# Dealing row pairs in turn to sixteen partition groups in a SwiGLU kernel: a 16 x 8 access pattern in place of 128 rows

## The chip, the cores and the metric

The kernel runs on one core of one Trainium2 chip. The metric is the device time of one execution in microseconds. Before the change the median is 936.3 us (936.06 to 936.35 in three runs). The kernel moves 268.44 MB from HBM into SBUF and 134.22 MB back, so it is a question of transfers almost alone (the two queues' shares of sixteen engines' span, 68.6 and 31.2%, add up to 99.8%). In this program HBM is the memory that holds x and out; SBUF is the one that holds the tiles, 128 partitions (rows) on which SiLU and the multiply work. A transfer (DMA) between the two is issued from a queue, here SP's or ACT's. The profile's page reckons the shares of the queues on sixteen DMA engines, and the records show each transfer as packets: here one packet is the run of one partition (3,968 load packets of 65,536 bytes, 31 loads of 128 partitions). A transfer has landed when its last packet is in place.

Runs are sorted by a rule into fast and slow: a run over 1.5% above the fastest of the same kernel counts as slow. A ratio is the mean time of one kernel's fast runs over that of the kernel before's fast runs in the same rounds, so it is not quite the ratio of the medians that I quote. Where only one run of a kernel counts as fast there is no ratio.

## The reference

```python
def reference(x):                     # x: [8192, 8192] float32
    a, b = np.split(x, 2, axis=-1)
    silu_b = b / (1 + np.exp(-b))
    return a * silu_b                 # [8192, 4096] float32
```

## The kernel before

A tile takes 256 rows. Each of the 128 partitions holds two neighbouring rows, 64 KiB of x in one run, and writes two result rows, 32 KiB of out in one run. Three such tiles fill 192 KiB of each partition. Loads are issued from the SP queue, stores from the ACT queue, the last ones from SP.

```python
    R = 2
    BUFS = 3
    xv = x.tensor.reshape([N // R, R * M]).ap()         # row pairs of x, 64 KiB each
    ov = out.tensor.reshape([N // R, R * half]).ap()    # row pairs of out, 32 KiB each
    ntiles = N // (P * R)                               # 32
    ...
    def load(i, rows=None):
        ...
        nc.sync.dma_start(
            out=tiles[i][:, lo * M : hi * M], in_=xv[i * P : (i + 1) * P, lo * M : hi * M]
        )
    ...
    def store(i, c0=0, cw=R * half):
        (nc.scalar if i < last - 1 else nc.sync).dma_start(
            out=ov[i * P : (i + 1) * P, c0 : c0 + cw], in_=tiles[i][:, c0 : c0 + cw]
        )

    for i in range(BUFS):
        load(i)
    for i in range(last):
        for k in range(R):
            swiglu(i, k)          # SiLU in place on ACT, then the multiply on DVE
        ...
        store(i)
        nxt = i + BUFS
        if nxt < last:
            load(nxt)
    ... # the last tile is loaded in two halves and stored in two halves
```

## Time and profile before

| | kernel before |
|---|---|
| span in the profile | 934.8 us |
| 64 KiB load packet, median of the packet records | 2.42 us |
| 32 KiB store packet, median of the packet records | 1.21 us |

The prediction below shows the engine totals, the queues, the chain and the stretches. Here are the rates of the forty slices and the issues of the large transfers from the page of the kernel before. In an issue line the last number is the median time from issue to landing.

```profile
GB/s 404 400 445 430 430 439 433 428 435 443 428 430 439 429 442 432 435 426 453 419 430 452 411 452 423 428 447 425 433 433 453 414 443 429 426 447 428 425 437 376
...
out_dram<-xt ACTq DMA_DIRECT2D x30, 4096.0 KB, 39.7
...
xt<-in_x_dram SPq DMA_DIRECT2D x31, 34.5
```

The first two slices, nearly all loads (the first store packet starts at 39.5 us, the slices end at 46.7), run at 404 and 400 GB/s; after that the rate stands near 433. A load takes 34.5 us to land. The middle of the run handles one tile in 29.0 us (for example, the chain's loads start at 98.96, 185.89 and 272.94 us, three tiles apart). So when the next load is issued, only some 34.5 - 29.0 = 5.5 us of loading is still queued (my estimate).

### The profile page before, as it was taken

Reading aid. Unit: us, or ns where it says so; the run is one execution under the profiler, and the core shown is the slowest. Engines: PE = TensorE matmul, PEld = TensorE weight load, DVE = VectorE, ACT = ScalarE, POOL = GpSimd, SP = SyncE. Lnnn points to the kernel's source line nnn. Section 1 sums busy time; section 2 is a strip of 40 time slices with the busy share of each in tenths; the row PEclk is TensorE's granted clock in tenths of the full one; section 3 lists DMA queues with packets and bytes.
Section 4 is the critical chain, followed back from the end, with each engine's and each line's share of the span. In section 5 each row is a group of like instructions: output and inputs, shape, how many; then the busy total and the mean of one; then the engine's idle time right before and its main releaser. Section 6 shows DMA issues by size and latency. Waiting matters only on the chain.

```text
span 934.8 us, 367 instructions
## 1 busy us (share of the span) xinstructions
DVE 283.3 (30%) x65; ACT 229.4 (25%) x66; POOL 0.2 (0%) x4
## 2 busy tenths in 40 slices
DVE  0333312333123331133321333213332133331242
ACT  0223320233302333113331133311333203332041
POOL 0000000000000000000000000000000000000000
DMA  9999999999999999999999999999999999999998
GB/s 404 400 445 430 430 439 433 428 435 443 428 430 439 429 442 432 435 426 453 419 430 452 411 452 423 428 447 425 433 433 453 414 443 429 426 447 428 425 437 376
DMA packets 9506, 402.67 MB, mean 431 GB/s; under 512 B 1056, under 2 KB 1056, under 8 KB 1056
## 3 DMA queue, kind: packets, MB, share of 16 engines
q1 hardware_dynamic: 5184, 276.83, 68.6%
q10 hardware_dynamic: 4320, 125.83, 31.2%
q14 instruction: 2, 0.02, 0.0%
HBM read 268.44 MB, written 134.22 MB: 431 GB/s over the span
## 4 chain that ended last, share of the span: by engine, by line
DMA 84%; DVE 10%; ACT 4%; DVEq 0%; issue 0%; SPq 0%; ACTq 0%
DMA out_dram<-xt 42%; DMA xt<-in_x_dram 42%; DVE xt L51 10%; ACT xt L50 4%; DVEq L106 0%; SPq L43 0%; ACTq L50 0%; DVEq L51 0%
## 5 line engine op out<-in xcount | busy, mean ns | idle before, releaser
L51 DVE TENSOR_TENSOR xt<-xt 128x4096 f32<-128x4096 f32 (+1 forms) x65 | 283.3, 4359 | 637.7 <-ACT xt L50 634.5
L50 ACT ACTIVATE xt<-xt 128x4096 f32<-128x4096 f32 (+1 forms) x65 | 228.1, 3556 | 688.1 <-DMA xt<-in_x_dram 688.1
L50 ACT ACT_TABLE_LOAD x1 | 1.3, 1283 | 0.7 <-PEq L95 0.7
L95 POOL MEMSET const-bfloat16-1.0<- 128x1 bf16 x1 | 0.1, 103 | 0.0
L95 POOL MEMSET const-uint8-127<- 128x1 uint8 x1 | 0.1, 102 | 0.0
L95 POOL MEMSET const-float32-0.0<- 128x1 f32 x1 | 0.1, 100 | 0.2 <-issue 0.2
L95 POOL MEMSET const-float32-1.0<- 128x1 f32 x1 | 0.1, 99 | 0.0
## 6 DMA issues: line engine op xcount, KB each, us to landing
out_dram<-xt ACTq DMA_DIRECT2D x30, 4096.0 KB, 39.7
xt<-in_x_dram SPq DMA_DIRECT2D x2, 4096.0 KB, 27.1
out_dram<-xt SPq DMA_DIRECT2D x1, 4096.0 KB, 23.6
out_dram<-xt SPq DMA_DIRECT2D x2, 2048.0 KB, 14.5
xt<-in_x_dram SPq DMA_DIRECT2D x31, 34.5
```

The source lines that it names most:

```text
L50: nc.scalar.activation(out=b, in_=b, func=_SILU)
L51: nc.vector.tensor_mul(out=xt[:, k * half + c0 : k * half + c0 + cw], in0=xt[:, k * M + c0 : k * M + c0 + cw], in1=b,)
L95: nc = _bacc.Bacc("TRN2", target_bir_lowering=False, num_devices=1)
```

## The change

The intent is to bring together in HBM what is read at the same moment. Before, a partition group of eight reads eight consecutive row pairs, so groups are 512 KiB apart in x and 256 KiB apart in out. After, consecutive row pairs are dealt in turn to the sixteen groups, so groups are 64 and 32 KiB apart. Each partition still has one 64 KiB run and one 32 KiB run per tile, and the result is the same.

```diff
-    xv = x.tensor.reshape([N // R, R * M]).ap()
-    ov = out.tensor.reshape([N // R, R * half]).ap()
     ntiles = N // (P * R)
+    G = 16
+    xv = x.rearrange("(i j e r) m -> i e j (r m)", i=ntiles, e=G, r=R)
+    ov = out.rearrange("(i j e r) m -> i e j (r m)", i=ntiles, e=G, r=R)
...
-            out=tiles[i][:, lo * M : hi * M], in_=xv[i * P : (i + 1) * P, lo * M : hi * M]
+            out=tiles[i][:, lo * M : hi * M], in_=xv[i, :, :, lo * M : hi * M]
...
-            out=ov[i * P : (i + 1) * P, c0 : c0 + cw], in_=tiles[i][:, c0 : c0 + cw]
+            out=ov[i, :, :, c0 : c0 + cw], in_=tiles[i][:, c0 : c0 + cw]
```

In the built program this does two things at once. The HBM addresses change, and the HBM side of each transfer becomes a pattern of 16 x 8 rows instead of 128 rows. The second was not the intent.

## The prediction

A "pair" is two engines that hinder each other when they work on like packets at the same moment ("in step"), each then taking twice as long. That was an assumption; no trace had shown it. So were two others: that a pair's lag at the start would last, and that a lag of four packets would cost nothing. The sum of the forecast came to 188 + 558 + 560 = 1,306, rounded to 1,300 us. All three terms can be read below (the case without cost: 937 to 950 us, taken as 942 in the first term), and the ground of the other two is the assumption just named. "HBM aliasing" stands for load packets that grow longer by the spacing of the addresses; no trace had shown that either. The chance of 0.01 for a gain of over 2% rested on the ceiling; what the trace shows is 433 GB/s with the engines occupied for 99.8% of the span.

> **What bounds the kernel now.** I read the engine totals first, then the slices, the queues, the chain that ended last, and last a table of stretches, to see whether some part of the run is unlike the rest.
>
> ```profile
> DVE 283.3 (30%) x65; ACT 229.4 (25%) x66; POOL 0.2 (0%) x4
> ...
> DMA  9999999999999999999999999999999999999998
> ...
> DMA packets 9506, 402.67 MB, mean 431 GB/s; under 512 B 1056, under 2 KB 1056, under 8 KB 1056
> ## 3 DMA queue, kind: packets, MB, share of 16 engines
> q1 hardware_dynamic: 5184, 276.83, 68.6%
> q10 hardware_dynamic: 4320, 125.83, 31.2%
> ```
>
> The compute engines work 30% and 25% of the span, while the DMA row is full in every slice. The two queues together occupy 68.6 + 31.2 = 99.8% of sixteen engines' span: 933 of 934.8 us. Nothing that shortens a wait can give more than the missing 2 us; only faster packets could.
>
> How fast are the packets? Queue 1 holds 0.686 x 16 x 934.8 = 10,260 engine-us for 276.83 MB, 27.0 GB/s per engine; queue 10 holds 4,667 engine-us for 125.83 MB, also 27.0 GB/s. One queue mostly reads HBM, the other only writes it, and their rates are equal. The single packet records say it more sharply: a 65,536-byte load packet takes 2.42 us at the median, a 32,768-byte store packet 1.21 us, and only 38 of the 8,192 row packets are over 20 ns longer than the usual time for their size, most of them at the first tile or near 49 us. [...]
>
> ```profile
> by line: DMA out_dram<-xt 42.5%; DMA xt<-in_x_dram 41.5%; DVE xt L51 9.7%; ACT xt L50 4.1%; issue 0.2%; DVEq L106 0.2%; SPq L43 0.1%; ACTq L50 0.0%; DVEq L51 0.0%
> ```
>
> The chain of waits passes load, SiLU, two multiplies, store, and back to the load that needed the buffer. Its 14% of compute is no gain in reserve: other tiles' transfers fill the engines in that time.
>
> ```profile
> 60.00:500.00 440.00, 132.76 (x30) 106.84 (x30) 0.00 (x0) 1.00 1.00 433
> 500.00:890.00 390.00, 115.05 (x26) 94.60 (x27) 0.00 (x0) 1.00 1.00 433
> 890.00:935.00 45.00, 17.77 (x5) 12.44 (x5) 0.00 (x0) 1.00 0.93 399
> ```
>
> In these lines the last two columns are the DMA share and GB/s. The middle of the run is even: 433 GB/s with the engines wholly occupied.
>
> [...]
>
> **The change, part by part.** The instruction order on all engines is unchanged: 33 loads, 33 stores, 65 SiLUs and multiplies, the same sizes and waits. A partition still holds one 64 KiB run of x and writes one 32 KiB run of out, so I expect the same 8,192 row packets and 9,506 in all, and 0 us for compute and issue.
>
> What is meant to change is which HBM rows are read together. That can remove at most the excess of slow packets: summed over the 38 and divided by 16 engines, it is 2.2 us. So the gain side is worth 0 to 2 us.
>
> What the change also does, beside the pitch, is to alter the form of the access pattern. In the built kernel the DRAM side is no longer 128 rows but 16 x 8 rows, against 128 partitions in SBUF. [...]
>
> The cost depends on how far a pair is out of step. In the steady part an engine alternates one load packet L (2.42 us) and one store packet S (1.21 us): 3.63 us, 256 such pairs being the floor of 929 us. I assume [...] that only like meets like. Then:
> - in step: L takes 4.84 and S 2.42, 7.26 for 3.63, twice the time: 929 x 2 = 1,858, about 1,865 us with the ends.
> - out of step by a lag between S and L, 1.2 to 2.4 us: L covers 2/3 of each period, so two L's overlap for at least 1/3 of it, 1.21 us, which adds 1.21: 4.84 for 3.63, times 1.33: about 1,240 us.
> [...]
>
> [...] The packets of the first wave start within 0.8 us of each other, and a lag of 0.5 us costs (7.26 - 1.0)/3.63 = 1.72. Over hundreds of packets lags should drift, and the slowest pair sets when a tile has landed. [...]
>
> **The rivals.**
> - Nothing happens: [...] the pairs drift fully apart at once. For it: the kernel already overlaps three tiles with no barrier between packets, and the first wave (packets up to 3.47 us) settled to 2.42 us after one packet. [...] It gives 934 to 950 us; chance 0.2.
> - HBM aliasing: [...] If it came anyway, load packets alone 5 to 20% longer would add 0.05 to 0.2 x 600 = 30 to 120 us (600 being 3,968 load packets x 2.42 / 16): 965 to 1,055. Chance of it alone about 0.1.
> - The change gains what its author hoped: at most 2 us, to 934; under 2% in any case.
> - Transfer issue becomes dearer with three dimensions: the store issue takes 0.34 us on ACT's queue now; doubled over 33 stores it is 11 us, off the path while other packets are queued. It moves nothing.
>
> **Range and chances.** I weigh no meeting 0.2 at 942 us, the 1.33 case (with weaker meeting or aliasing beside it) 0.45 at 1,240, and near step 0.35 at 1,600: 188 + 558 + 560 = 1,306, rounded to 1,300 us. The distribution has two humps, and the range must reach both: 940 to 1,750. Faster by over 2% would need 917 us, or 402.65 MB at 439 GB/s[...]: 0.01. Within 2%: 0.19. Slower: 0.80.
>
> **What would show it.** Right: packets and bytes the same, DMA row still full, SiLU and multiply as long as now (3.6 and 4.4 us), but load packets of 3 to 4.8 us and stores of 1.6 to 2.4 us in the records, steady GB/s of 220 to 330, and long packets all through the run rather than a few at its start. [...] Times of 2.42 and 1.21 throughout prove the first rival[...]. A packet count other than 9,506 would show that the rows are cut differently, which I have not counted on. The prediction fails most cheaply at the lag: if pairs separate by themselves within a few tiles, the answer is some 945 us[...].

## The result, and the profile after

The changed kernel takes 1,548.22 us in the median of six runs (1,513.63 to 1,560.27) against 936.24 us. The ratio of the fast runs is 1.626 (1.615 to 1.638). The result is correct.

The profile fell on the longest of the six runs (span 1,558.5 us). These lines are from the page of the changed kernel: engine totals, the DMA row of the slices and their rates, the queues, and the issues.

```profile
DVE 283.2 (18%) x65; ACT 229.4 (15%) x66; POOL 0.2 (0%) x4
...
DMA  9999999999999999999999999999999999999997
GB/s 215 215 267 278 254 259 258 262 267 262 252 259 272 256 262 275 241 272 253 277 254 264 254 264 266 267 246 268 255 271 257 266 248 275 249 272 259 262 243 236
DMA packets 9506, 402.67 MB, mean 258 GB/s; under 512 B 1056, under 2 KB 1056, under 8 KB 1056
...
q1 hardware_dynamic: 5184, 276.83, 77.9%
q10 hardware_dynamic: 4320, 125.83, 21.6%
...
out_dram<-xt ACTq DMA_DIRECT2D x30, 4096.0 KB, 59.7
...
xt<-in_x_dram SPq DMA_DIRECT2D x31, 71.9
```

Compute is unchanged to 0.1 us, and so are the packets and the bytes, to the packet. The DMA row is as full as before. A busy share therefore tells nothing here: the engines are occupied in both kernels, but the packets last longer. The loads' queue pays most: 68.6% of 934.8 us was 641 us of each engine, 77.9% of 1,558.5 is 1,214 us. The stores' queue went from 292 to 337 us. Those two add 573 + 45 = 618 us, nearly the whole 624 us by which the spans differ.

In the packet records a 64 KiB load packet now takes 4.64 us on average, 1.92 times the former 2.42. A 32 KiB store packet on the ACT queue takes 1.40 us, 1.16 times the former 1.21. The first two slices, loads alone until the first store packet at 67.3 us, are the plainest reading: 215 GB/s, about half of the 404 and 400 GB/s of the same slices before and of the 433 of the middle of that run. In them the load packets after the first wave take about 5.1 us, 2.1 times the former 2.42. (A slice counts a packet whole where it starts; sixteen packets of 65,536 bytes in 5.12 us are 205 GB/s.)

The table of stretches of the changed kernel (last two columns: DMA share and GB/s) shows that the loss is even over the run:

```profile
60.00:300.00 240.00, 44.24 (x10) 35.61 (x10) 0.00 (x0) 1.00 1.00 262
600.00:900.00 300.00, 53.10 (x12) 42.73 (x12) 0.00 (x0) 1.00 1.01 263
1200.00:1500.00 300.00, 61.95 (x14) 48.56 (x14) 0.00 (x0) 1.00 1.00 261
```

The chain of waits is of no use in this profile. It gives 94% to a releaser that it can't name:

```profile
another core or an unknown queue 94%; DMA 3%; SPq 1%; ACT 0%; DVE 0%; DVEq 0%; issue 0%; ACTq 0%
```

There is no other core in this program. The SP queue's own waits are readable instead (waited for, us in total, times, longest):

```profile
SPq L44 <- DMA out_dram<-xt: 1443.8, 29, 110.3
```

Loads still wait for the stores that free their buffers, as before, where the same wait was:

```profile
SPq L43 <- DMA out_dram<-xt: 869.3, 29, 67.8
```

No new wait was formed; the same loop turns more slowly.

### The profile page after: what moved, and what is told of

The parts are those of the page before. It is cut to its first block, busy times and chain, and to the rows that moved or that the text cites. A ratio compares the mean times of both kernels' runs of the same rounds, so it can differ in the third digit from the quotient of the medians.

```text
span 1558.5 us, 367 instructions
## 1 busy us (share of the span) xinstructions
DVE 283.2 (18%) x65; ACT 229.4 (15%) x66; POOL 0.2 (0%) x4
## 2 busy tenths in 40 slices
DMA packets 9506, 402.67 MB, mean 258 GB/s; under 512 B 1056, under 2 KB 1056, under 8 KB 1056
## 3 DMA queue, kind: packets, MB, share of 16 engines
q1 hardware_dynamic: 5184, 276.83, 77.9%
## 4 chain that ended last, share of the span: by engine, by line
another core or an unknown queue 94%; DMA 3%; SPq 1%; ACT 0%; DVE 0%; DVEq 0%; issue 0%; ACTq 0%
DMA xt<-in_x_dram 3%; SPq L44 1%; ACT xt L51 0%; DVE xt L52 0%; DVEq L107 0%; ACTq L51 0%
## 6 DMA issues: line engine op xcount, KB each, us to landing
out_dram<-xt ACTq DMA_DIRECT2D x30, 4096.0 KB, 59.7
```

## The experiments

My theory was that in the 16 x 8 form DMA engines hinder each other in pairs when they work at the same moment, and that HBM has no part in it. The trace names no engine per packet, and no run shows where engines meet. What the runs can test is whether the form or the addresses cost the time, and whether the timing between engines does. The main rival was the HBM spacing, which the change was about.

### Undo the spacing, keep the form

The pattern stays 16 x 8 on both sides, but each group reads the eight pairs that lie together, at the old spacing. The order inside a group is reversed, only so that the two dimensions are not merged back into 128.

```diff
-    xv = x.rearrange("(i j e r) m -> i e j (r m)", i=ntiles, e=G, r=R)      # and ov likewise
+    def pairs(t, i, w, c0, cw):
+        return bass.AP(tensor=t.tensor, offset=(i * P + 7) * w + c0,
+                       ap=[[8 * w, G], [-w, 8], [1, cw]])
...
-            in_=xv[i, :, :, lo * M : hi * M]
+            in_=pairs(x, i, R * M, lo * M, (hi - lo) * M)                    # and the store likewise
```

Expected:

> The 16 x 8 form on both sides is kept, but HBM has the old spacing: group e of partitions reads the eight row pairs that lie together at 512 KiB pitch in x and 256 KiB in out (each group from its last pair to its first, so that the two dimensions are not merged into 128). [...] nothing changes against the changed kernel, 1,500 to 1,560 us, load packets of 4.6 us. HBM spacing (rival): back to the kernel before, 934 to 955 us, load packets of 2.42 us. Both at work: something between, 1,000 to 1,450.

Measured: correct, 1,514.1 us in the median of four runs (1,440.3 to 1,552.3). Only the run at 1,440.3 counts as fast, so there is no ratio; the slowest of the kernel before took 936.59 in the same rounds. Its profile, of a run of 1,547.6 us, has these rates:

```profile
GB/s 217 217 259 276 272 254 265 259 275 259 255 270 257 281 259 277 254 270 258 273 270 256 262 258 266 270 256 266 257 274 264 254 270 252 275 259 263 261 254 226
```

The row is the changed kernel's over again, with 217 GB/s in the first two slices. Load packets average 4.59 us and stores 1.40. Restoring the spacing of the groups restores nothing beyond the scatter of the runs. One gap is left. Which rows the engines of the kernel before read at one moment is not shown, and they need not be spaced quite as here; the next run narrows this gap for the loads.

### Keep the plain form, take the small spacing

Here the kernel before is kept, with 128 rows, but the step between the runs of two partitions in x is 16 KiB in place of 64. The runs overlap in HBM, so the result is wrong.

```diff
-            in_=xv[i * P : (i + 1) * P, lo * M : hi * M]
+            in_=bass.AP(tensor=x.tensor, offset=i * P * R * M + lo * M,
+                        ap=[[M // 2, P], [1, (hi - lo) * M]])
```

Expected:

> The kernel before with its plain 128-row form, but the step from one partition's run to the next in x is 16 KiB instead of 64, so the runs overlap[...]; the result is wrong on purpose. [...] 934 to 945 us with load packets of 2.42 us. HBM spacing (rival): [...] 1,400 us or more, load packets over 4 us.

Measured: 935.35 us (two runs), ratio 0.999 (0.997 to 1.001). Load packets average 2.425 us. The rates of its slices:

```profile
GB/s 404 404 449 425 428 447 428 438 432 442 428 424 441 428 444 431 438 417 455 429 420 445 425 455 421 430 447 411 448 427 435 438 430 427 432 458 413 430 441 388
```

This is the row of the kernel before. A limit of this run: it reads each stretch of HBM several times and leaves the stores as they were, so it clears a small spacing of the loads and not, by itself, that of out; and which rows are read at the same moment, no record shows. Together with the run above it leaves the form of the pattern as the cause: the new form at the old spacing took 1,514.1 us, the old form at a small spacing 935.35. So the HBM rival falls for the loads, and the loads carry nearly the whole cost, as the next runs show.

### Half of the change: loads only, stores only

Two kernels take one half of the change each. Their rows come out permuted, so both results are wrong.

```diff
 # loads only: the changed kernel, with the stores of the kernel before
-    ov = out.rearrange("(i j e r) m -> i e j (r m)", i=ntiles, e=G, r=R)
+    ov = out.tensor.reshape([N // R, R * half]).ap()
-            out=ov[i, :, :, c0 : c0 + cw]
+            out=ov[i * P : (i + 1) * P, c0 : c0 + cw]
 # stores only: the same for xv and the load
```

Expected of the loads-only kernel:

> Loads as in the changed kernel, stores as in the kernel before; rows come out permuted, so the result is wrong on purpose. In the changed kernel load packets took 4.64 us and store packets 1.40 on the ACT queue, so loads alone hold 1,150 of its 1,550 us. If the loads pay nearly all: 4.6 to 4.85 us a load packet and 1.21 a store, in all 1,460 to 1,530 us. If sharing were paid by both kinds alike as my model had it (x1.33 to x2 of each): 930 + 600 x (0.33 to 1) = 1,130 to 1,530, which does not separate from the first, but the store packets at 1.21 do. If the spacing of out were at fault: near 936.

Measured: 1,496.9 us (1,470.4 to 1,539.7), ratio 1.582 (1.569 to 1.596). Its profile has:

```profile
GB/s 201 225 290 293 292 283 276 274 298 297 296 283 290 267 271 298 275 288 260 254 274 274 256 274 254 269 258 268 258 261 266 263 263 259 271 265 262 264 265 272
```

The loads carry nearly the whole cost: 1,496.9 - 936.0 = 561 us of the 612 us. The reading of the stores needs care: in this kernel they have the plain form and still take 1.36 us. So nearly all of what stores lose in the changed kernel (1.40 us for 1.21) comes with the slow loads, and only 0.04 us is left for their own form. Why a slow load lengthens a store no run shows. The row also shows something that I had not expected. After the first two slices the rate stands mostly between 270 and 298 GB/s for a third of the run, and it sinks to some 265; load packets average about 4.05 us in the third tenth of the run and 4.6 in the seventh. I read this as engines that fall into step by degrees; the records name no engine, so this run does not show it.

Expected of the stores-only kernel:

> Loads as in the kernel before, stores as in the changed kernel; rows permuted, the result wrong on purpose. If stores of a pair of engines met in step and paid double: store packets of 2.4 us, 610 + 2 x 320 = 1,250 us. If they pay as in the changed kernel, 1.40 us each: 610 + 337 + 20 = 965 us. If stores pay only when no load is beside them (the last stores of the changed kernel took 2.1 us on average, with no load left): 940 to 950 us.

Measured: 1,012.6 us (991.9 to 1,018.5; four runs). Store packets average 1.37 us and scatter up to 4.5; load packets average 2.53. Stores in the new form cost 76 us, about an eighth of the whole. The two halves add up to 561 + 76 = 637 us against 612 for both, the same within the scatter of these runs. The value lies above what I had forecast for mild sharing (965) and far below full sharing (1,250). The third alternative in that text rested on a misreading: of the 384 packets of 32 KiB on the SP queue in the changed kernel, 256 are half-tile loads and not stores, so their 2.1 us said nothing about stores alone. The packets do not settle: stores average 1.27 us in the first tenth of the run and 1.47 in the last.

### Stores alone

To see stores without loads, three plain loads fill the buffers and all 32 stores of the new form follow from them (wrong result).

```diff
     for i in range(BUFS):
         load(i)                       # plain form
-    for i in range(last):
+    for i in range(BUFS):
         for k in range(R):
             swiglu(i, k)
-        ...
+    for i in range(ntiles):
+        tiles[i] = tiles[i % BUFS]
+        store(i)                      # 16 x 8 form
```

Expected:

> Three plain loads, then all 32 stores of the changed kernel's form from those three buffers with no loads between; the result is wrong on purpose. [...] If stores of a pair halve each other: 2.4 us a store packet, 58 + 256 x 2.42 + 12 = 690 us. [...] 1.21 us, 58 + 311 + 12 = 380 us.

Measured: 422.1 us (two runs), between the two answers. The slices, of 10.5 us each, say why:

```profile
GB/s 398 398 455 442 398 399 296 361 389 336 249 252 249 296 271 330 333 358 389 411 436 427 423 445 436 411 448 433 414 448 427 420 448 411 436 448 411 427 318 65
```

The loads have landed at 62 us. Until 104 us two of the 32 stores, which the kernel issues from SP, run beside those of the ACT queue (296 to 389 GB/s). Then the ACT queue's stores are alone and run at some 250 GB/s, with packets of up to 2.81 us, and recover by themselves to 410 to 450 GB/s, with packets of 1.22 us. So stores in this form are slowed with no load beside them, and they recover in about 100 us (from 249 GB/s near 105 us to 411 near 200) and stay fast. I read this as engines that get out of step by themselves.

The loads of the loads-only run went the other way, from 4.05 to 4.6 us a packet. That need not be a difference between the directions, because the stores here are also queued far deeper:

```profile
out_dram<-xt ACTq DMA_DIRECT2D x30, 4096.0 KB, 77.8
```

One takes 77.8 us to land, while a 4 MiB store at the 433 GB/s of the kernel before would take 9.7 (my estimate). In the stores-only run, where each store waits for its tile, the packets did not recover (1.27 us in the first tenth, 1.47 in the last). The depth of the queue, which the last experiments below test for loads, is a rival that no run on stores rules out.

### Does being in step cost the time? A lag given at the start

If the cost comes from what engines do at the same moment, then putting them out of step should remove it although the form is unchanged. I used tiles of one row per partition (half as long packets, six buffers), and put two small loads before the first tile, one of twelve groups and one of four, with four rows a group, meant to make some engines start the tile later than others. The trace shows such groups: in the run with three buffers below, the sixteen semaphore rises of the third load come as four, eight and four, with about 5 and 7 us between. That a lag of four packets is wholly out of step, and one of two half way, was my assumption; no run shows why.

```diff
-    R = 2
-    BUFS = 3
+    R = 1
+    BUFS = 6
 # the lag, before the first load (4, or 2 with a partition step of 4; absent in the base):
+    xl = x.rearrange("(a e) m -> e a m", e=G)
+    for m, k in enumerate((12, 4)):
+        nc.sync.dma_start(out=tiles[BUFS - 1][m : m + 8 * k : 2, :],
+                          in_=xl[:k, m * 4 : (m + 1) * 4, :])
 # then one plain loop over the 64 tiles: swiglu, store, next load
```

Expected of the base without a lag, of a lag of two, of a lag of four, and of the control in the plain form:

> The changed kernel with one row per partition and tile (32 KiB load packets, 16 KiB store packets, six buffers instead of three, no special last tiles). It is the base for the two runs with a lag, chosen because its half as long packets need half the lag in time. [...] pairs in step: load packets of 2.3 us instead of 1.21, 1,450 to 1,580 us. If smaller packets and more buffers let pairs drift apart by themselves: 1,000 to 1,300.

> As the run with one row, but before the first tile [...] (loads of 12 and of 4 groups into the buffer that is filled last; the result stays correct). A pair then starts half way out of step[...]. If the lag that a pair starts with lasts (my prediction's assumption): loads pay about half, 930 + 0.5 x 540 = 1,200 us. If pairs fall back into step: as the run without lag. If they separate further by themselves: under 1,050.

> The same with four packets more: a pair starts wholly out of step[...]. If the lag lasts: no meeting, 945 to 1,000 us, load packets of 1.21 us. If something draws pairs into step again: a fast start and then packets of 2.3 us, 1,300 to 1,560 us. [...] the lag changes nothing: as the run without lag.

> The control: one row per partition and tile, six buffers, but the plain 128-row form of the kernel before[...]. 935 to 950 us, load packets of 1.21 us. If it is slower than 955, one row per partition has a cost of its own that the other three carry too.

Measured, all correct and in the same rounds:

| one row, six buffers | median of four (range), us | ratio | mean load packet, us |
|---|---|---|---|
| plain form (control) | 941.8 (941.6 to 941.8) | 1.006 | 1.22 |
| 16 x 8, no lag | 1,342.9 (1,330.6 to 1,360.9) | 1.430 | 1.86 |
| 16 x 8, lag of two | 1,327.4 (1,318.2 to 1,332.4) | 1.417 | 1.82 |
| 16 x 8, lag of four | 1,073.9 (1,049.9 to 1,225.6) | 1.127 | 1.43 |

The profile of the lag of four fell on a run of 1,088 us.

The rates of the slices, first of the control, then of the kernel without a lag:

```profile
GB/s 396 425 425 428 435 435 431 431 441 425 434 435 434 427 439 428 427 441 429 432 430 437 431 435 430 433 436 430 432 428 439 430 432 430 436 431 435 430 433 324
...
GB/s 203 281 292 294 301 307 307 320 312 310 317 293 315 312 308 278 315 311 312 317 310 304 315 308 303 308 308 305 315 301 309 305 299 312 300 298 309 300 300 174
```

And of the kernel with a lag of four, with its landing times:

```profile
GB/s 246 337 383 393 384 380 385 392 393 384 388 389 370 367 377 362 371 378 382 399 390 380 387 389 384 383 392 384 375 384 386 377 375 388 383 372 386 369 366 199
...
xt<-in_x_dram SPq DMA_DIRECT2D x64, 4096.0 KB, 56.7
```

With a lag of four the kernel moves 2 MB more, has the same form and the same addresses for its tiles, and is 269 us faster. Two thirds of the cost over the control (401 us) are gone (by the ratios, 0.303 of 0.424), and the higher rate lasts to the end of the run. Apart from the extra packets nothing but the timing between engines has changed, so this timing is the cause of that part. Where engines meet the lag doesn't say: that it isn't in HBM rests, for the loads, on the two runs on spacing (1,514.1 and 935.35 us), and what they share, and which engine with which, was not shown. One of the four runs took 1,225.6 us, so the state is not safe. The lag of two gained 15 us where I had forecast half of the cost: a missed forecast. Its load packets take 2.47 us already between 10 and 40 us, against 2.48 without a lag, so this small lag gained next to nothing even at the start.

Without a lag the kernel was already better than I expected (1,343 us instead of 1,450 or more). Its load packets fall from 2.48 us between 10 and 40 us to 1.84 after 100 us: with six buffers the packets recover in part by themselves, as engines that get out of step would.

### The same lag in the changed kernel, and the number of buffers

Expected of the changed kernel itself, two rows and three buffers, with a lag of four of its packets (the same added lines, with row pairs in place of rows):

> The changed kernel itself (two rows, three buffers) with the lag of four packets between the engines of a pair set before the first tile; the result stays correct. With long packets the lag is four times 3.6 us, 14.5 us. In the kernel before, a load is issued every 29.0 us and takes 34.5 us to land, so when the next load is issued only some 5.5 us of work is queued, and the engine that leads would run dry and lose its lead. If queued work limits the lag: about 1.5 of 4 packets of lag survive, loads pay some 60%: 1,200 to 1,400 us. If the lag lasts whole: 950 to 1,080. If it is lost at once: 1,480 to 1,560.

Measured: correct, 1,480.4 us (1,449.4 to 1,489.8; four runs). The profile fell on the longest run:

```profile
GB/s 227 386 378 275 294 300 310 298 287 277 278 273 293 279 279 264 249 274 271 258 262 256 267 259 258 255 271 266 257 250 270 265 256 267 248 267 257 264 247 242
```

The second and third slices, 37 us each, stand at 386 and 378 GB/s. Then the rate falls to 275 and by the middle of the run to about 260. Mean load packets per tenth of the run (from the first record on) go 3.31, 3.98, 4.18, 4.35, 4.61 us and stay there. By these lengths the engines began out of step, as intended, and fell back into step. My reckoning of 1.5 surviving packets (1,200 to 1,400 us) was too kind; the time met the third forecast, of a lag lost at once, by a hair, although the lag held for some 106 us.

Two explanations remained: the three buffers (too little queued work for a leading engine to stay ahead) or the long packets. So I took the good run with one row and a lag of four, and changed only the number of buffers from six to three, with a control in the plain form.

```diff
-    BUFS = 6
+    BUFS = 3
```

> The run with one row and a lag of four packets (1,074 us with six buffers), with three buffers instead of six. In the plain control with six buffers a load took 53.9 us to land at a tile every 14.5 us, so some 39 us of work were queued against a lag of 4 x 1.82 = 7.3 us. With three buffers next to nothing is queued. If queued work is what keeps a pair apart: the lag is lost as with two rows, 1,250 us or more, a fast start and then a fall of the rate. If the packet length decides and not the queued work: 1,050 to 1,120 us as with six buffers, plus what the control shows.

> The control for the run before: one row per partition, three buffers, plain 128-row form[...]. 940 to 990 us, load packets of 1.21 us; what it has over 942 us is the cost of fewer buffers alone.

Measured: 1,460.8 us with the lag (1,456.4 to 1,472.5; ratio 1.562), 944.7 us in the control (943.7 to 951.9; ratio 1.009). The first slices of the run with the lag, and its landing times:

```profile
GB/s 266 314 290 287 291 284 268 286 277 280 282 268 286 278 272 279 270 286 276 276 282 270 281 274 274 283 271 286 274 268 286 271 286 282 269 290 279 274 286 198
...
xt<-in_x_dram SPq DMA_DIRECT2D x64, 4096.0 KB, 28.6
```

Packet length and lag are those of the good run; with three buffers the kernel is 387 us slower, while the control in the plain form pays 3 us for the same three buffers. (The six-buffer runs were on another chip; the kernel before took 936.2 us there and 936.1 here.) So here the number of buffers decides whether the gain of the lag is kept. One detail differs besides: the extra packets land in the buffer filled last, which is the third here and the sixth there, so one early load waits for them sooner. But the lag was set all the same: between 40 and 50 us the load packets average 1.48 us, against 1.52 with six buffers. I think a leading engine runs out of queued loads and has to wait for the one behind it, which lines them up again.

The semaphore rises in the trace agree with this. A load raises its semaphore sixteen times (in the kernel before 1,056 rises for 66 transfers), which I take to be once for each engine that has finished its share; the records name no engine. For the third load the rises come in groups that fit the two extra loads, of twelve groups and of four: four near 49.2 us, eight near 54.2, four near 61.4. The fourth load is the first that waits for a store to free its buffer, and it is issued at 59.7 us. By then twelve of the third load's rises were 5 to 10 us old, while four were still to come: as I read it, twelve engines without a load and four still busy. The fourth load's rises follow at 81.1 (four), 85.1 to 85.5 (eight) and 86.0 to 86.2 us (four), so the last two groups, 7 us apart before, are now less than 1 us apart. Load packets average 2.29 us between 60 and 70 us, against 1.38 with six buffers. The two-row run does the same: 2.42 us from 90 us until its fourth load is issued at 105.9 us, with twelve rises of the third load by 100.2 and four at 113, and 4.22 from there to 130 us.

No version here beats the kernel before. Its packets already run at a nearly constant 2.42 and 1.21 us, so rearranging rows had at most the 2 us of the prediction to win.

## Why the prediction was right or wrong

**The bound, and no gain from spacing: right.** The step that HBM spacing could give at most 2 us holds: a step of 16 KiB from partition to partition in the plain form made 935.35 us against 936.01.

**The unintended change of form: right in what it says about time.** Form without spacing costs about as much as the change (1,514.1 us), small spacing without form costs nothing (935.35), and loads alone fall to 215 GB/s. That engines hinder each other by their timing is supported by the lag of four (1,073.9 us for 1,342.9). Which engines do so and what they share, the ground of the prediction, was not shown. One reading was off by its time base: the slow packets "near 49 us" lie 36 to 41 us from the span's start, around the first store.

**Slower by over 2%: right.** The measured 1,548 us lies in the range, but 940 to 1,750 us is so wide that this says little. The point of 1,300 us, a mean of three cases and none of them itself, was too low by 248 us, and that comes from two terms.

**The mis-sized term: the weights of the three cases.** The text put 0.35 on "near step" at 1,600 us and 0.65 on cases at 1,240 or 942. Measured load packets of 4.64 us stand at 1.92 of the 2.0 that the model gives to a pair in step: by the model, the two-row kernel has its loads in step nearly all the time. (Beside no stores they even take about 5.1 us, more than the model's 4.84; no run says why.) The assumption behind the weights, that a lag lasts and over time drifts, failed. With three buffers and two rows the gain of a lag is gone by the middle of the run (load packets of 3.31 us in its first tenth, 4.61 in its fifth); with six buffers and short packets, that of a lag of four mostly stays (1,073.9 us) and one of two gains next to nothing (1,327.4 for 1,342.9). What undoes a lag with few buffers is, by my reading of the semaphore rises, the wait for the next load, which the model didn't have.

**"Only like meets like", with loads and stores paying alike: wrong for stores.** In step, the model had 4.84 for a load and 2.42 for a store, 7.26 us in place of 3.63. Measured are 4.64 and 1.40, 6.04 us. And 256 x 6.04 = 1,546 us, within 1% of the profiled run's 1,558.5. Full meeting describes the loads and fails for stores beside loads. That the near-step case at 1,600 us comes so close is luck in part: it stood for partial meeting of both kinds, and what happened is full meeting of one. I had listed stores of 1.6 to 2.4 us as a sign of being right; at 1.40 that sign failed.

**The rivals.** "Nothing happens" fell, and so did HBM aliasing, for the loads (how it would show in the packet times was assumed). Dearer issue was there and cost nothing: the store issue on ACT's queue went from 0.34 to 0.56 or 0.62 us in the timeline, off the path. The text's warning that pairs might separate came true for stores alone and in part with six buffers, and the opposite for loads with three, if packet lengths tell it (1.22 us at the end for stores alone, 1.84 after 100 us for loads with six buffers, 4.61 with three); by what means, no run shows.

## What to carry to other kernels

An access pattern chose here not only addresses but also how long packets took (4.59 us a load packet in the 16 x 8 form at the old spacing, 2.425 in the plain form at a small one). So a layout change should be tested in two halves: the new addresses in the old form, and the old addresses in the new form. A full DMA row with unchanged packet counts is no proof of full speed: both kernels show the row full and 9,506 packets, at 936 and 1,548 us. The mean time of one packet of a known size tells it (2.42 against 4.64 us), and where it was already constant, rearranging HBM rows gained nothing here. Where the layout allows it, try first to keep 128 partitions as one plain dimension on the HBM side: the 16 x 8 form cost a factor of 1.63 here. Where packets were slowed by each other's timing, six buffers in place of three kept most of the gain of a lag (1,074 us against 1,461, with one row per partition).
